# Output projection and gate as products of 64 rows, each group in its own bank over two slots

## The chip, the cores and the metric

The kernel runs on one core of a Trainium2 chip. The metric is the device time of one execution in microseconds. The engines are named as in the profile: PE (TensorE, matrix products), PEld (its weight loads), DVE (VectorE), ACT (ScalarE), POOL (GpSimd) and SP (SyncE, which issues DMAs).

## What is computed

One encoder layer over two sequences of 2048 rows of 1024 channels, with shared weights:

```python
u = _rmsnorm(h, g_norm)
z = u @ w_in
q, k, v, ga, f, gf = jnp.split(z, [int(c) for c in cuts], axis=-1)
...
a = _blocked_gqa(q, k, v) * jax.nn.silu(ga)
fo = _fourier_branch(f, w_fmix) * jax.nn.silu(gf)
h = h + jnp.concatenate([a, fo], axis=-1) @ w_out
gate = jax.nn.sigmoid(_rmsnorm(h, g_ple) @ w_ple_gate)
return h + (p @ w_ple) * gate
```

A final RMSNorm follows. Attention has 8 query heads over 2 key heads of 64 channels, without a mask.

## The kernel before

**Numbers.** A matrix product of fp32 accuracy is made of three fp16 products: each operand is split in a high and a low half, and `SPLIT3` names the pairs high x high, high x low, low x high. The helper `mm` (L433 is its matmul) runs 8 slices of 128 contracted channels times 3 products, 24 matmuls of 128 rows by 512 columns, into one PSUM bank: that is a **group**. The embedding product p @ w_ple has 2 slices, 6 matmuls.

**Stages.** First the input projection (`project`), up to some 834 us. Then attention (`attention`), a list of turns that `interleave` runs through, with a generator of other work (`fill`: the Fourier branch, then `outp`) between them. At last what is left of `outp`.

**A turn.** 64 units (sequence, key head, block of 128 queries) have 8 turns each. A turn holds six score products of 64 rows (L1126; rows 0-63 and 64-127 of PE side by side, each half in a bank of its own), two products of the running maxima for a later unit (L1153, 64 rows), then DVE's reduction of these (L1161) and ACT's two exponentials (L1129), which the scores of the turn after must wait for. Every fourth turn is heavy: it has the second attention products (L1191, 128 rows by 64 columns). In one turn of eight the sums (L1225) come, in another `max_rows` (L1177). After that the turn takes work from `fill` until its budget is spent; a generator that yields None ends its turn. `FILL` is the total that the budget is spread over. DVE work is put off by `defer` to the flush at the start of the next turn, longer DVE work by `defer_slow` to the heavy turns.

**The output projection** (`outp`), for each of 32 tiles of 128 rows: `out1` twice (the product with w_out, halves n = 0 and 1, from mh and its transposed part mT) and DVE's residual addition (L1371); `square` (ACT, L1400) and `norm`; `out2` scales the rows (ACT L1429, DVE L1433) and transposes them by DMA into hT; `out3` twice (the gate's product with w_ple_gate, ACT's tanh at L1380, the embedding product, and DVE's two operations, L1387 and L1388); a second `square`, then `out4`. The loop works on out1 of tile t, out3 of t - 1 and out4 of t - 2. `split` makes mh (ACT L1351, DVE L1356) and mT (DMA).

**Banks.** During attention the scores, maxima and second products have five of the eight PSUM banks. Three, the pool `psF`, go round among the groups, the embedding products, the sums and `max_rows`. `psX` holds five more before and after attention.

## Time and profile before

| | us |
|---|---|
| median of 3 runs | 2769.4 |
| lowest, highest | 2768.34, 2774.16 |
| the profiled execution | 2765.67 |
| its span, first to last instruction | 2763.9 |

The profile is of one execution. A row in order of time has its start, its length, engine, line and operation, the tile written and read, the shape and the number of merged instructions; matmul lengths contain the pipeline's end, so a distance between starts tells PE's rate. A wait in brackets names the idle time before and who ended it.

### The profile page before, as it was taken

Reading aid. Unit: us, or ns where it says so; the run is one execution under the profiler, and the core shown is the slowest. Engines: PE = TensorE matmul, PEld = TensorE weight load, DVE = VectorE, ACT = ScalarE, POOL = GpSimd, SP = SyncE. Lnnn points to the kernel's source line nnn. Section 1 sums busy time; section 2 is a strip of 40 time slices with the busy share of each in tenths; the row PEclk is TensorE's granted clock in tenths of the full one; section 3 lists DMA queues with packets and bytes.
Section 4 is the critical chain, followed back from the end, with each engine's and each line's share of the span. In section 5 each row is a group of like instructions: output and inputs, shape, how many; then the busy total and the mean of one; then the engine's idle time right before and its main releaser. Section 6 shows DMA issues by size and latency. Waiting matters only on the chain.

```text
span 2763.9 us, 40442 instructions
## 1 busy us (share of the span) xinstructions
PE 2674.9 (97%) x15332; PEld 1181.3 (43%) x15332; DVE 1684.7 (61%) x2467; ACT 1211.4 (44%) x2047; POOL 1630.8 (59%) x1394
## 2 busy tenths in 40 slices
PE   6899999999998989999999999999999999999998
PEld 3465655656555543333333333333333333333333
DVE  6755555654555766666666666665665665666645
ACT  3443333332224544445444544444444444444442
POOL 1233233433336697777768777777667766777770
PEclk9999999999999999999999999999999999999999
DMA  7467676774528752122222223222222222222223
GB/s 231 143 190 190 191 197 169 191 173 111 149 74 245 225 172 67 48 73 71 56 60 54 56 72 93 73 60 63 64 68 55 67 74 61 54 69 77 56 54 92
DMA packets 418532, 296.37 MB, mean 107 GB/s; under 512 B 259456, under 2 KB 360000, under 8 KB 418336
## 3 DMA queue, kind: packets, MB, share of 16 engines
q1 hardware_dynamic: 405424, 252.01, 35.0%
q0 software_dynamic: 12912, 41.77, 4.5%
q8 instruction: 120, 1.97, 0.3%
q14 instruction: 76, 0.62, 0.1%
HBM read 149.50 MB, written 86.51 MB: 85 GB/s over the span
## 4 chain that ended last, share of the span: by engine, by line
PE 78%; DVE 3%; issue 3%; DMA 2%; POOL 1%; ACT 1%; SPq 0%; DVEq 0%; POOLq 0%; ACTq 0%
PE ps_f L433 31%; PE ps_o L1191 15%; PE ps_s L1126 14%; PE ps_x L433 9%; PE ps_m L1153 4%; PE ps_f L1225 1%; PE ps_f L1177 1%; PE ps_f L1045 1%; PE ps_f L999 1%; ACT p L1129 1%; DMA hT<-h_hl 0%; DMA w_st<-in_w_out 0%; DVE a_mx L1161 0%; DMA g_in<-gd 0%; DMA w_st<-in_w_ple_gate 0%
## 5 line engine op out<-in xcount | busy, mean ns | idle before, releaser
L1134 POOL TENSOR_TENSOR acc<-acc,p 128x1024 f32<-128x1024 f32 x384 | 911.6, 2374 | 248.5 <-ACT p L1129 181.4
L1129 ACT ACTIVATE p<-ps_s,s_scale 128x512 f32<-128x512 f32 x1024 | 647.4, 683 | 753.6 <-PE ps_s L1126 736.9
L1161 DVE TENSOR_REDUCE a_mx<-ps_m 128x1 f32<-128x1024 f32 x499 | 610.2, 1223 | 593.5 <-PE ps_m L1153 592.8
L1191 PE MATMUL ps_o<-p,v 128*64 128x512 f32 x2048 | 467.5, 599 | 0.0
L433 PEld LDWEIGHTS <-uc 128*128 128x128 f16 x3072 | 301.1, 98 | 312.2 <-issue 22.5
L1126 PE MATMUL ps_s<-q,k 64*128 64x512 f16 x3072 | 424.7, 380 | 4.6 <-ACT p L1129 4.5
L433 PE MATMUL ps_f<-w_pg,hT 128*128 128x512 f16 x1464 | 351.1, 382 | 6.4 <-DMA hT<-h_hl 6.2
L1191 PEld LDWEIGHTS ps_o<-p,v 128*64 128x64 f32 x2048 | 142.2, 138 | 258.1 <-issue 249.2
L1126 PEld LDWEIGHTS <-k 64*128 64x128 f16 x3072 | 116.0, 94 | 305.1 <-issue 234.0
L433 PEld LDWEIGHTS <-hT 128*128 128x128 f16 x1536 | 138.9, 98 | 211.5 <-issue 61.0
L1132 POOL TENSOR_TENSOR acc<-p,p 128x1024 f32<-128x1024 f32 x64 | 150.5, 2352 | 111.2 <-ACT p L1129 111.1
L1153 PE MATMUL ps_m<-k,q 64*128 64x512 f16 x998 | 192.9, 378 | 16.8 <-DVE a_mx L1161 15.5
L433 PE MATMUL ps_f<-w_wo,mh 128*128 128x512 f16 x744 | 181.9, 381 | 4.6 <-DVE mh L1356 4.5
L433 PE MATMUL ps_f<-w_wo,mT 128*128 128x512 f16 x744 | 180.9, 380 | 0.0
L433 PEld LDWEIGHTS <-w_ga 128*128 128x128 f16 x1536 | 150.1, 99 | 44.1 <-issue 15.0
L915 POOL DMA_DIRECT2D gfd<-gt x32 | 19.2, 601 | 213.3 <-DVE gt L943 208.4
L1207 ACT ACTIVATE tb<-ps_o,a_scale 64x256 f32<-64x256 f32 x128 | 60.0, 469 | 165.2 <-PE ps_o L1191 164.4
L433 PE MATMUL ps_x<-uc,w_ga 128*128 128x256 f16 x1008 | 114.8, 275 | 3.8 <-ACT ge L900 3.1
L1227 DVE RECIPROCAL ps_f<-ps_f 128x256 f32<-128x256 f32 x64 | 112.4, 1756 | 7.2 <-PE ps_f L1225 7.2
L433 PEld LDWEIGHTS <-mh 128*128 128x128 f16 x768 | 68.7, 98 | 107.9 <-issue 33.2
L433 PEld LDWEIGHTS <-mT 128*128 128x128 f16 x768 | 70.0, 98 | 98.7 <-issue 25.9
L933 POOL DMA_DIRECT2D agd<-gat x64 | 35.8, 559 | 127.8 <-DVE gat L943 127.7
(283 smaller groups left out, 3322.9 us busy)
## 6 DMA issues: line engine op xcount, KB each, us to landing
q<-qTd SPq DMA_DIRECT2D x256, 64.0 KB, 2.2
ag<-agd SPq DMA_DIRECT2D x64, 256.0 KB, 4.5
out<-h POOLq DMA_DIRECT2D x31, 512.0 KB, 4.0
x<-in_x_prompt SPq DMA_DIRECT2D x16, 512.0 KB, 5.2
w_st<-in_w_out SPq DMA_DIRECT2D x32, 256.0 KB, 4.4
gfd<-gt POOLq DMA_DIRECT2D x32, 256.0 KB, 3.3
gd<-ge POOLq DMA_DIRECT2D x32, 256.0 KB, 3.4
agd<-gat POOLq DMA_DIRECT2D x64, 128.0 KB, 2.4
```

What stands on the lines that cost most here:

```text
L433: self.nc.tensor.matmul(ps, lhs(ia, k), rhs(ib, k), start=(i == 0), stop=(i == 3 * ks - 1))
L933: nc.gpsimd.dma_start(self.agd[s][1, r * 128:(r + 1) * 128, c * n:(c + 1) * n], gt[:, :n])
L999: nc.tensor.matmul(o, fT[:, r, y, :], self.bd[:, y, r, :], start=True, stop=x is None)
L1126: nc.tensor.matmul(S[u][e][:], w[sl], q[sl].rearrange("p h q -> p (h q)"), start=j == i == 0, stop=i + 1 == len(todo), skip_group_check=True)
L1129: nc.scalar.activation(p[:, e, :], S[u][e][:], AF.Exp, scale=self.sc["s_scale"][:])
L1132: nc.gpsimd.tensor_tensor(out=ACC[u][:], in0=P[u, 0][:], in1=p[:], op=ALU.add)
L1134: nc.gpsimd.tensor_tensor(out=ACC[u][:], in0=ACC[u][:], in1=p[:], op=ALU.add)
L1153: nc.tensor.matmul(ps[c], Q[u][0][sl, h, :], kt[s, kv, half][sl, :, 0, :], start=True, stop=True)
L1161: nc.vector.reduce_max(MX[u][:, h, half, c:c + 1], x, axis=AX.X)
L1191: nc.tensor.matmul(o[64 * e:64 * e + 64, :], vt[s, kv, c // 8][:, c % 8, :], p[:, e, :], start=(j == 0), stop=(j == 7))
L1207: nc.scalar.activation(tb[64 * e:64 * e + 64], ov[64 - 64 * e:128 - 64 * e, e], AF.Copy, scale=self.sc["a_scale"][64 - 64 * e:128 - 64 * e ...
L1227: nc.vector.reciprocal(r, ps[:, 0:256])
```

## The change

A group no longer runs as 24 products of 128 rows. Each product is cut into its upper 64 rows and its lower 64 rows. In one slot (`slot`, `halves`) the upper products of a new group alternate with the lower products of the group before it. Each group keeps its own bank over both slots, so it is finished a slot later than its upper half. After attention, when `psX` is there again, groups run whole.

- `psF` has one bank, the new pool `psG` two. Once `outp` has begun (`grouped`), groups take `psG`; sums, `max_rows` and embedding products take `psF`. Before that, `bank` goes round over the three as it did.
- `out1` and `out3` return the two operands and what follows the group, which runs after its lower half. The residual addition is no longer put off.
- A slot gives way after 6, 9, 12, 15, 18 and 24 steps (before: after every 3 matmuls) and ends its turn's filling with its end.
- `middle` does both squares and `norm`; `late` (out2 and out4) follows four turns later (`due`, `poll`); the loop waits for it where it needs the result (`wait`).
- `FILL` is 775 instead of 755.

```diff
-FILL = 755.0
+FILL = 775.0
...
-O4 = 6
+STOPS = (6, 9, 12, 15, 18)
...
-        self.psF = ep(tc.tile_pool(name="psF", bufs=3, space=PSUM))
+        self.psF = ep(tc.tile_pool(name="psF", bufs=1, space=PSUM))
+        self.psG = ep(tc.tile_pool(name="psG", bufs=2, space=PSUM))
+        self.grouped = False
...
         self.nx += 1
-        if self.psX is not None and self.nx % 8 < 5:
-            return self.psX.tile([128, 512], F32, name="ps_x")
-        return self.psF.tile([128, 512], F32, name="ps_f")
+        if self.grouped:
+            p, n = (self.psF, "ps_f") if self.psX is None else (self.psG, "ps_g")
+        elif self.psX is not None and self.nx % 8 < 5:
+            p, n = self.psX, "ps_x"
+        else:
+            p, n = (self.psF, "ps_f") if self.nx % (8 if self.psX is not None else 3) % 5 == 2 else (self.psG, "ps_g")
+        return p.tile([128, 512], F32, name=n)
+
+    def group_bank(self):
+
+        p, n = (self.psX, "ps_x") if self.psX is not None else (self.psG, "ps_g")
+        return p.tile([128, 512], F32, name=n)
...
+        def slot(up):
+
+
+            low = held.pop() if held else None
+            if low is not None and (low[4] or self.psX is not None):
+                j = st.tile([128, 1], F32, name="seen")
+                nc.vector.tensor_copy(j[:], low[0][:, 0:1])
+            if up is not None and self.psX is None:
+                up = (self.group_bank(), *up, not started)
+                started.append(True)
+                held.append(up)
+                yield from halves(up, low)
+            else:
+                if low is not None:
+                    yield from halves(None, low)
...
+        def halves(up, low):
 
+            i = n = 0
+            for k in range(8):
+                for ia, ib in SPLIT3:
+                    for g, sl, a, z in ((up, slice(0, 64), i == 0, False), (low, slice(64, 128), False, i == 23)):
+                        if g is not None:
+                            nc.tensor.matmul(g[0][:], g[1](ia, k)[sl], g[2](ib, k)[sl], start=a, stop=z,
+                                             skip_group_check=True)
+                    i += 1
+                    if i in STOPS:
+                        yield 0.216 * (i - n)
+                        n = i
+            n = self.nflush
+            more = low[3](low[0]) if low is not None else None
+            yield 0.216 * (24 - STOPS[-1])
+            if more is not None:
+                more()
+                yield 1.48
+            if self.dq is not None and self.nflush == n:
+                yield None
...
+        def middle(t):
+
+            ss = st.tile([128, 2], F32, name="h_ss")
...
+            if ok(t - 2):
+                yield from self.after(TK[t - 2])
+                square(t - 2, 1, ss)
+                PT.pop(t - 2)
+                HT.pop(t - 2)
+            if ok(t):
+                square(t, 0, ss)
+            q, r = norm(ss)
+
+            def late():
+                if ok(t):
+                    tk[t] = out2(t, q)
+                if ok(t - 2):
+                    t4[t - 2] = out4(t - 2, r)
+
+            due.append((self.nflush + 4, late))
```

**What stands in a row now.** On PE, in a light turn in the midst of attention, from the maxima on. Names are `k`, `q` (attention), `hT` (rows for the gate), `mh` (rows for the output projection), `w_pg`, `w_wo` (weights). Before:

```order
L1153 MATMUL ps_m<-k_7165,q_13005 128x512 [waits DVE_49]
L1153 LDWEIGHTS q_13005 [waits DMAHW7_49]
L1153 MATMUL ps_m<-k_7165,q_13005 128x512
L433 LDWEIGHTS hT
L433 MATMUL ps_f<-w_pg_9874,hT 128x512
```

And now:

```order
L1164 MATMUL ps_m<-k_7168,q_12396 128x512 [waits DVE_49]
L1164 LDWEIGHTS q_12396
L1164 MATMUL ps_m<-k_7168,q_12396 128x512
L1445 LDWEIGHTS hT [waits DMAHW1_49]
L1445 MATMUL ps_g<-w_pg_9388,hT 128x512
L1445 LDWEIGHTS mh
L1445 MATMUL ps_g<-w_wo_8988,mh 128x512
```

Where one group's load and product repeated, a gate group's upper half (rows 0-63) and an output group's lower half (rows 64-127) alternate, in two banks of `ps_g`.

On PE, in a turn with `max_rows` that follows a turn with an embedding product. Before:

```order
L1153 MATMUL ps_m<-k_7168,q_13005 128x512 [waits DVE_49]
L1153 LDWEIGHTS q_13005
L1153 MATMUL ps_m<-k_7168,q_13005 128x512
L1177 MATMUL ps_f<-ident,nm 128x128
L433 LDWEIGHTS mh
L433 MATMUL ps_f<-w_wo_8660,mh 128x512 [waits Activation_49]
```

And now:

```order
L1164 MATMUL ps_m<-k_7171,q_12973 128x512 [waits DVE_49]
L1164 LDWEIGHTS q_12973
L1164 MATMUL ps_m<-k_7171,q_12973 128x512
L1188 MATMUL ps_f<-ident,nm 128x128 [waits DVE_49]
L1445 LDWEIGHTS mh
L1445 MATMUL ps_g<-w_wo_8988,mh 128x512
```

The product of `max_rows` now waits for DVE; what it waits for in the built program is the second operation on the embedding product (L1407), which reads the same bank.

On ACT, around the squares of a tile in the second half of attention (`p` are the exponentials, `th` the tanh, `tb` a copy after a heavy turn, `nm` the negated maxima). Before:

```order
L1380 ACTIVATE th<-ps_f,h_pg_6890 128x512
L1129 ACTIVATE p_16180<-ps_s,s_scale 128x512 x2
L1400 ACTIVATE h_hl,h_ss<-h 128x1024
L1129 ACTIVATE p_16241<-ps_s,s_scale 128x512 x2
L1207 ACTIVATE tb<-ps_o,a_scale 64x256 x2
```

And now:

```order
L1182 ACTIVATE nm<-a_m_17107 128x2x4
L1466 ACTIVATE sq,h_ss<-h 128x1024
L1466 ACTIVATE h_hl,h_ss<-h 128x1024
L1140 ACTIVATE p_17241<-ps_s,s_scale 128x512 x2
L1140 ACTIVATE p_17267<-ps_s,s_scale 128x512 x2
```

The two squares of a step of the loop stood at two places, with exponentials between them, and stand together now.

## Rows read from the trace of the kernel before

**Rows 1.** The profile's page: busy time, the granted clock of TensorE in 40 slices, and the chain that ended last, by engine and by line.

```profile
PE 2674.9 (97%) x15332; PEld 1181.3 (43%) x15332; DVE 1684.7 (61%) x2467; ACT 1211.4 (44%) x2047; POOL 1630.8 (59%) x1394
...
PEclk9999999999999999999999999999999999999999
...
PE 78%; DVE 3%; issue 3%; DMA 2%; POOL 1%; ACT 1%; SPq 0%; DVEq 0%; POOLq 0%; ACTq 0%
PE ps_f L433 31%; PE ps_o L1191 15%; PE ps_s L1126 14%; PE ps_x L433 9%; PE ps_m L1153 4%; PE ps_f L1225 1%; PE ps_f L1177 1%; PE ps_f L1045 1%; PE ps_f L999 1%; ACT p L1129 1%; DMA hT<-h_hl 0%; DMA w_st<-in_w_out 0%; DVE a_mx L1161 0%; DMA g_in<-gd 0%; DMA w_st<-in_w_ple_gate 0%
```

**Rows 2.** Busy time by stretch: attention with the Fourier branch, attention with the output projection, the rest. After the stretch and its length, the busy us of each engine (and its instructions), TensorE's granted clock, the DMA share and GB/s.

```profile
834.00:1062.00 228.00, 202.53 (x1343) 110.06 (x1340) 142.33 (x179) 116.36 (x193) 170.16 (x108) 0.95 0.65 199
1062.00:2690.00 1628.00, 1613.75 (x8990) 577.58 (x8989) 1012.79 (x1047) 783.99 (x1304) 1183.37 (x1007) 1.00 0.25 64
2690.00:2764.00 74.00, 64.17 (x298) 27.98 (x295) 39.15 (x88) 16.97 (x26) 10.89 (x10) 0.95 0.37 91
```

**Rows 3.** PE in order of time: a light turn and the start of the heavy turn after it.

```profile
1341.21 0.82 PE L1126 MATMUL ps_s<-q,k 64*128 64x512 f16 x6
1341.87 0.38 PE L1153 MATMUL ps_m<-k,q 64*128 64x512 f16 x2
1342.18 2.12 PE L433 MATMUL ps_f<-w_pg,hT 128*128 128x512 f16 x9
1344.23 0.82 PE L1126 MATMUL ps_s<-q,k 64*128 64x512 f16 x6
1344.89 0.38 PE L1153 MATMUL ps_m<-k,q 64*128 64x512 f16 x2
1345.20 0.65 PE L1225 MATMUL ps_f<-acc,ones 128*64 128x256 f32 x4
```

**Rows 4.** PE in order of time after attention: a whole group of the gate and what follows it.

```profile
2704.80 5.34 PE L433 MATMUL ps_f<-w_pg,hT 128*128 128x512 f16 x24
2709.98 1.46 PE L433 MATMUL ps_x<-wp,pT 128*128 128x512 f16 x6
```

**Rows 5.** PE in order of time in the input projection: two groups of 256 columns.

```profile
485.75 2.78 PE L433 MATMUL ps_f<-uc,w_ga 128*128 128x256 f16 x24
488.37 2.78 PE L433 MATMUL ps_x<-uc,w_ga 128*128 128x256 f16 x24
```

**Rows 6.** PE in order of time: the start of a turn and its `max_rows`, and later an embedding product at the end of a turn and the start of the next.

```profile
1324.04 0.82 PE L1126 MATMUL ps_s<-q,k 64*128 64x512 f16 x6
...
1325.00 0.49 PE L1177 MATMUL ps_f<-ident,nm 128*128 128x128 f32 x2
...
1329.64 1.46 PE L433 MATMUL ps_f<-wp,pT 128*128 128x512 f16 x6
1331.03 0.39 PE L1126 MATMUL ps_s<-mr,kone 64*128 64x512 f16 x2
```

**Rows 7.** DVE in order of time in the same turns: the reduction, the reading of the `max_rows` bank, and the two operations on the embedding product.

```profile
1325.12 1.23 DVE L1161 TENSOR_REDUCE a_mx<-ps_m 128x1 f32<-128x1024 f32 x1 [1.15 <-PE ps_m L1153]
1326.26 0.68 DVE L1179 TENSOR_TENSOR mr<-ps_f,own 128x512 f16<-128x512 f32 x1
...
1331.20 0.70 DVE L1387 SCALAR_TENSOR_TENSOR ps_f<-th,ps_f 128x512 f32<-128x512 f32 x1 [1.53 <-PE ps_f L433]
1331.93 0.75 DVE L1388 SCALAR_TENSOR_TENSOR h<-ps_f,p_wp,h 128x512 f32<-128x512 f32 x1
```

**Rows 8.** ACT in order of time: a square with the reading of its accumulator and the exponentials behind it, and the exponentials of the turn that starts at 1344.23.

```profile
1338.05 1.05 ACT L1400 ACTIVATE h_hl<-h 128x1024 f16<-128x1024 f32 x1
1339.00 0.20 ACT L1400 ACTIVATION_READ_ACCUMULATOR h_hl<-h 128x1 f32 x1
1339.09 1.26 ACT L1129 ACTIVATE p<-ps_s,s_scale 128x512 f32<-128x512 f32 x2
...
1345.15 1.26 ACT L1129 ACTIVATE p<-ps_s,s_scale 128x512 f32<-128x512 f32 x2 [1.75 <-PE ps_s L1126]
```

**Rows 9.** PE in order of time at the start of attention: the first score product of three turns, two of them without filling.

```profile
835.56 0.37 PE L1126 MATMUL ps_s<-q,k 64*128 64x512 f16 x1 [0.54 <-ACT p L1129]
...
837.52 0.37 PE L1126 MATMUL ps_s<-q,k 64*128 64x512 f16 x1 [0.36 <-ACT p L1129]
...
839.48 0.37 PE L1126 MATMUL ps_s<-q,k 64*128 64x512 f16 x1 [0.36 <-ACT p L1129]
```

**Rows 10.** Who waited for whom from 1066 to 2690 us: us in total, times, longest.

```profile
PEld L433 <- DMA hT<-h_hl: 9.7, 7, 3.0
...
PE ps_f L433 <- DMA hT<-h_hl: 6.2, 4, 2.5
...
PE ps_f L433 <- DVE mh L1356: 4.5, 3, 1.7
```

**Rows 11.** One of DVE's groups by line and shape, the residual addition, from 1100 to 2650 us: busy us, mean ns of one, idle time before.

```profile
L1371 DVE SCALAR_TENSOR_TENSOR h<-ps_f,mixo,h 128x512 f32<-128x512 f32 x54 | 40.2, 745 | 4.2 <-PE ps_f L433 4.2
```

**Rows 12.** The end of the program in order of time: the last product and the last output.

```profile
2752.71 1.46 PE L433 MATMUL ps_x<-wp,pT 128*128 128x512 f16 x6
...
2760.24 1.00 SPq L1421 DMA_DIRECT2D out<-h  x2
```

More of the change, by code (lines that the diff above doesn't have):

```diff
@@ new lines, in slot @@
+        def slot(up):
[11 more added lines that the diff above has]
+                    yield from halves(None, low)
+                if up is not None:
+                    ps = self.group_bank()
+                    yield from self.mm(ps[:], up[0], up[1])
+                    more = up[2](ps)
+                    if more is not None:
+                        more()
+                        yield 1.28
@@ new lines, in halves @@
+        def halves(up, low):
[13 more added lines that the diff above has]
+            yield 0.216 * (24 - STOPS[-1])
+            if more is not None:
+                more()
+                yield 1.48
+            if self.dq is not None and self.nflush == n:
+                yield None
@@ L1459, in along, with poll, wait @@
             for us in g:
-                next(pr, None)
+                for _ in range(round(us / 0.648) if us else 0):
+                    next(pr, None)
+                poll()
                 yield us
+        def poll():
+            while due and (self.dq is None or self.nflush >= due[0][0]):
+                due.pop(0)[1]()
+        def wait(d, t):
+            while t not in d:
+                yield None
+                poll()
+            yield from self.after(d.pop(t))
+        def middle(t):
+            ss = st.tile([128, 2], F32, name="h_ss")
+            if not (ok(t) and ok(t - 2)):
+                nc.gpsimd.memset(ss[:], 1.0)
+            if ok(t - 2):
[12 more added lines that the diff above has]
+            due.append((self.nflush + 4, late))
+            if self.dq is None:
+                poll()
         mix = []
@@ L1476, in outp @@
         load_x(0)
-        t4, tm = [-1], []
+        held, started, due, tm, tk, t4 = [], [], [], [], {}, {}
+        self.grouped = True
         for t in range(N2 + 2):
-            ss = st.tile([128, 2], F32, name="h_ss")
-            if not (ok(t) and ok(t - 2)):
-                nc.gpsimd.memset(ss[:], 1.0)
             pr = prep(t + 1) if ok(t + 1) else iter(())
             if ok(t):
-                yield from along(out1(t, 0), pr)
-            if ok(t - 2):
-                yield from self.after(tf)
-                square(t - 2, 1, ss)
-            if ok(t):
-                yield from along(out1(t, 1), pr)
+                yield from along(slot(out1(t, 0)), pr)
+                if t == 1:
+                    yield from middle(0)
+                yield from along(slot(out1(t, 1)), pr)
+                load_p(t)
@@ L1506, in outp @@
-            if self.dq is not None and ok(t - 1):
-                yield from self.after(tn, 3)
-            if o4:
-                t4 = out4(t - 2, r)
-            if ok(t - 1):
-                PT.pop(t - 1)
-                HT.pop(t - 1)
-                tf = TK[t - 1]
-            if t == 0:
-                for _ in range(4):
-                    yield None
-            if ok(t):
-                tk = out2(t, q)
+                yield from wait(tk, t - 1)
+                yield from along(slot(out3(t - 1, 0)), pr)
+            elif t:
+                yield from along(slot(None), pr)
@@ L1519, in outp @@
+            if t:
+                yield from middle(t)
+            if ok(t - 1):
+                yield from along(slot(out3(t - 1, 1)), pr)
             if ok(t + 1):
-                yield from self.after(t3)
+                if ok(t - 3):
+                    yield from wait(t4, t - 3)
                 load_x(t + 1)
```

59 lines of the change are left out of this document (25 added, 34 removed).

## Prediction

> **What bounds the kernel now.** I read the page's first part and its chain before anything else [rows 1]: the TensorE (PE) is busy 97% of the span and the chain that ended last is 78% PE, while the next engine, DVE, stands at 61%. So only what shortens PE's row, or makes it wait, can move the time. Then the busy time by stretch [rows 2]: from 1062 to 2690 us, where attention and the output projection run side by side, PE is busy 1613.8 of 1628 us at a granted clock of 1.00 (the 2.4 GHz level). "Busy" is not yet "at its rate", since a matmul's end is modelled; so I went to PE's own rows in order of time [rows 3] and took the distance from start to start. In the last stretch 24 products of the gate take 5.18 us, 0.216 us each [rows 4]. In a turn of attention, 1341.21 to 1344.23, there are three steps of scores (six 64-row products, two side by side, 0.22 us a pair), one step of maxima (two side by side) and nine 128-row products: 13 steps of 0.216 us are 2.81 us, but the turn took 3.02. The 0.21 us left over lie at the two places where PE goes from 64-row to 128-row products and back: maxima to gate 0.31 instead of 0.22, and nine products in 2.05 instead of 1.94. **One change of form costs 0.106 us**, and no other engine is named there. That is what this change aims at.
>
> **Removed.** With 64-row products on both sides, scores, maxima and projection no longer differ in form. Counting the matmuls of both built programs, PE changes between 64-row, 128-row and 64-column forms 1044 times before and 582 times after. 462 x 0.106 = **-49.0 us**. What is left is at the attention's second products (L1191), the sums, the running maxima (L1177) and the embedding product (L433 wp), which keep their forms.
>
> **Added products.** 121 of the 128 groups become 24 upper and 24 lower halves. Of their 2928 steps 2880 hold a pair and 48 hold one half (the first group's upper rows, the last one's lower). Before, they were 121 x 24 = 2904 steps. 24 more x 0.216 = **+5.2 us**. I take a pair at 0.216, as the score pairs run [rows 3]. A pair issues two weight loads and two products. The nearest long run with that density is the 256-wide projection, 24 loads and 24 products in 2.62 us [rows 5], 0.109 for one load and one product, so 0.218 a pair: the upper end is 2880 x 0.002 = +6 us. Nothing makes a pair cheaper than its 0.216 of moving columns, so the lower end is 0.
>
> **The banks.** Before, sums, maxima, embedding and groups rotate through three banks. After, groups hold two for two slots and the other three share one. Whoever takes that one waits until DVE has finished with its last user.
> - Embedding at the end of a turn, then sums or maxima in the next: in the built order 16 times. The embedding ends with the turn; DVE's two operations on it start 0.17 us into the next turn (1331.20 against 1331.03) and end 1.65 us in [rows 6, 7]. Sums or maxima want the bank 0.96 us in [rows 6]. 0.73 x 16 = +11.7 us. Behind the waiting product stand the second products or the pairs of that turn, so nothing hides it.
> - Maxima, then an embedding in the same turn: 8 times. DVE reads the maxima's bank only after its reduction, until 2.90 us into the turn (1326.26 + 0.68, turn at 1324.04) [rows 6, 7]; four embeddings want it at 1.29 (wait 1.6 to 1.7), four at 2.69 (0.2 to 0.3): +7.7 us.
> - A group's bank: the next slot starts at the earliest 0.87 us into a turn, and the residual operation, 0.745 us on DVE [rows 11], cannot start before the group's last product ends, some 0.17 us in. That is 0.11 us late, at 31 places where a light turn goes straight to the pairs: +3.4 us; at no place less than 0, at all 45 +5.
>
> Together +22.8 us. Rows and rule can be weighed here. The rows show the three users of a shared bank and when DVE lets go of it. The Trainium skill, in TensorEngine Tiling (Array Packing), "Gotcha 1: PSUM Pressure", warns that row tiles raise the demand for banks, which speaks against taking the 49 us as the gain. Without the first two items, which are that pressure, the sum below would be 2731 us; with them it is what I forecast. No run here shows yet how large it is.
>
> **The scalar engine.** A turn's exponentials start 0.92 us in and end 2.18 us in [rows 3, 8], and the next but one turn's scores need them. A turn with no filling lasts 1.96 us [rows 9] though PE has only 0.87 us of work. Two edits bear on this. (1) The two squares, which stood at two places, now follow each other: 2 x 1.04 us (1338.05 to 1339.09) [rows 8]. For each pair of squares I compared 2.18 + 2.08 + 1.26 = 5.5 us with the length of its turn and the next, counted in steps: these are too short at five places, by 0.01 to 1.6 (there a copy of mh follows as well), in sum +3 us. Lower end 0, upper end the same pair at nine places, +9. (2) The group's end closes a turn's filling, and the waits for the normalised rows are by ticket: eleven light turns get no filling (or the running maxima alone), where six did before. 5 x 1.1 = +5.5 us (0 if the next turn's work covers it).
>
> **Weights of rows that come late.** PE's loads wait for hT seven times, 9.7 us, and its products for mh three times, 4.5 us [rows 10]. hT's second half is now issued at least two turns ahead but for the first tile, where eight were issued in the same turn or the one before: -9.7 us (0 if the transposing DMA is slower). mh's lower half is used in the turn in which it is made at five places instead of one in one and two in the next; at 1.5 us each (4.5 / 3) [rows 10] 7.5 instead of 4.5: +3.0.
>
> The tail keeps seven groups in 128-row form, and its last chain, from the last product at 2752.71 to the output [rows 12], is the same. FILL and the finer stops only set in which turn a product stands; that is in the counts above.
>
> **Sum.** -49.0 + 5.2 + 22.8 + 3 + 5.5 - 9.7 + 3.0 = -19.2 us. Against the profiled execution, 2765.7 us, that is 2746.5; that execution lies 3.7 us under the median of the runs, so the forecast is 2769.4 - 19.2 = **2750.2 us**.
>
> **Rivals.**
> - *The waits take it.* All waits at their upper ends: the second kind of bank wait always 1.66 (+5.6), nine pairs of squares (+6), 45 group banks (+1.6), hT as late as before (+9.7): 2773 us. For it: each engine has little slack in a light turn. Against it: DVE is at 61%, and a late PE gives ACT its time back.
> - *Waits overlap.* A wait at a bank also lets the exponentials catch up; half of the 34.3 us of new waits (22.8 + 3 + 5.5 + 3.0): 2733 us. For it: both sit in the same short turns. Against: the bank waits stand on PE's own path.
> - *Slower: a long run of pairs costs more than a score pair.* The rows show at most five pairs in a row; there the first pair costs 0.01 us more, three score steps taking 0.66 instead of 0.65 [rows 3]. If loads cannot keep ahead in runs of 6 to 12 pairs and every pair pays that 0.011, it is 2880 x 0.011 = +32 us: 2782 us. It decides from 19.2 / 2880 = 0.0067 us a pair on, where the gain is gone. Against it: [rows 5], where loads hold up at the same density. The Trainium skill, in TensorE: Matmul & The Clock Gate, "Wait — 56ns, not 53.3ns?", gives about 62 ns of sequencer work per matmul in one decoding mode; two are 124 ns and fit in a pair, but if loads paid it too, 248 ns a pair would be some 92 us more (an estimate from that page). The 109 ns for a load and a product in [rows 5] does not agree with that.
> - *It does not do what it says:* PE pays the change between upper and lower halves of different banks anyway. 2750.2 + 49 = 2799 us. The scores go to the maxima, other banks and other weights, with no such gap [rows 3].
>
> **How the numbers follow.** Forecast 0.61, waits at the upper end 0.12, overlap 0.20, slower pairs 0.05, no effect 0.02. A measurement here can tell about 0.2% (5.5 us) from no change. Faster by more: the forecast's and the overlap's chance but for a few hundredths, 0.80; within: most of the upper-end case, 0.13; slower: 0.07. The range leaves out the two slow cases, most of the upper end and the better half of the overlap: 2733 to 2767.
>
> **What would show it.** Light turns with pairs and no other form should last 13 steps, 2.81 us, not 3.02; a run of pairs should go at 0.216 each. The sums and maxima that follow an embedding should wait for DVE, 0.7 us each; embeddings after maxima 1.6. PE's waits for hT should be gone. I am wrong if a pair takes 0.22 or more, if a change of form still shows between maxima and pairs, or if PE's waits add up to far more or less than 35 us.

## Result: no gain, some 0.2% slower

| | before | after |
|---|---|---|
| median | 2770.3 us | 2776.0 us |
| lowest, highest | 2763.0, 2774.2 | 2772.5, 2778.6 |
| the profiled execution's span | 2763.9 | 2773.5 |

The ratio is 1.0022, 95% interval 1.0013 to 1.0032. The forecast was 2750.2 us in a range of 2733 to 2767: the time lies above the range, on the other side of no change.

**The profile after.** The page's first part and its chain, against [rows 1]: PE still sets the time, but DVE has grown from 3% to 7% of the chain.

```profile
PE 2656.9 (96%) x18236; PEld 1264.5 (46%) x18236; DVE 1684.4 (61%) x2469; ACT 1214.7 (44%) x2047; POOL 1636.9 (59%) x1394
...
PE 83%; DVE 7%; issue 3%; DMA 2%; POOL 2%; ACT 2%; SPq 0%; DVEq 0%; POOLq 0%; ACTq 0%
```

PE in order of time in a light turn, which answers to [rows 3]:

```profile
1849.35 0.81 PE L1137 MATMUL ps_s<-q,k 64*128 64x512 f16 x6
1849.99 0.38 PE L1164 MATMUL ps_m<-k,q 64*128 64x512 f16 x2
1850.21 0.38 PE L1445 MATMUL ps_g<-w_pg,hT 64*128 64x512 f16 x1
1850.21 0.38 PE L1445 MATMUL ps_g<-w_wo,mh 64*128 64x512 f16 x1
...
1851.94 0.38 PE L1445 MATMUL ps_g<-w_pg,hT 64*128 64x512 f16 x1
...
1852.15 0.81 PE L1137 MATMUL ps_s<-q,k 64*128 64x512 f16 x6
```

From scores to scores 2.80 us for 13 steps, where 3.02 stood before. From maxima to pairs 0.22, no longer 0.31. Nine pairs from 1850.21 to 1852.15, 0.216 each. The change does what it says, and the form changes are saved.

**Where the time went.** I cut both profiled executions at the first score product of attention and at that of its last turn. A step is one 128-row product or one pair of 64-row products. Losses are a turn's length less 0.216 us a step and 0.106 a form change, summed over the turns from PE's starts.

| us | before | after | difference |
|---|---|---|---|
| until attention (833.76, 844.80) | 833.8 | 844.8 | +11.0 |
| attention, 511 turns | 1854.2 | 1840.3 | -13.9 |
| of it steps and form changes | 1793.8 | 1745.0 | -48.8 |
| of it losses | 60.5 | 95.2 | +34.7 |
| from there to the end of the span | 75.9 | 88.4 | +12.5 |

Attention has the -49, and waits take 35 of it. But 23.5 us come in the two stages for which the sum had next to nothing: the projection ahead of attention, whose instructions are the same in the same order, and the tail.

PE's rows of who waited for whom from 1066 us to the end of attention, against [rows 10] (us in total, times, longest):

```profile
PE ps_s L1137 <- ACT p L1140: 6.5, 19, 0.7
...
PE ps_f L1236 <- DVE h L1407: 6.2, 8, 0.8
PE ps_f L444 <- DVE mr L1190: 6.0, 4, 1.5
...
PE ps_f L1188 <- DVE h L1407: 5.8, 9, 0.7
...
PE ps_g L1445 <- DVE mh L1367: 2.3, 4, 0.8
...
PE ps_g L1445 <- DMA hT<-h_hl: 2.2, 1, 2.2
```

The second to fourth are the one shared bank `ps_f`: 18.0 us in 21 waits, none of which stood in the trace before.

The projection, PE in order of time, and below it two stretches of 2 us (busy us of PE, PEld, DVE, ACT, POOL with their instructions, granted clock, DMA share, GB/s):

```profile
286.83 2.78 PE L444 MATMUL ps_g<-uc,w_ga 128*128 128x256 f16 x24
293.96 5.28 PE L444 MATMUL ps_g<-uc,w_ga 128*128 128x256 f16 x24 [4.35 <-DVE gat L954]
```

```profile
294.00:296.00 2.00, 2.00 (x10) 1.39 (x10) 0.96 (x2) 0.00 (x0) 0.54 (x1) 0.50 0.80 297
296.00:298.00 2.00, 2.00 (x12) 1.35 (x10) 0.00 (x0) 0.00 (x0) 0.00 (x0) 0.50 0.23 87
```

A group waits 4.35 us for DVE to read the group just before it, since both have the same bank of `ps_g`; then its 24 products take 5.28 us instead of 2.78, at a granted clock of 0.50 (the 1.2 GHz level).

The tail, PE and DVE in order of time, and PE's clock in the stretch:

```profile
2707.22 0.39 PE L444 MATMUL ps_x<-w_pg,hT 128*128 128x512 f16 x1
2710.57 8.16 PE L1445 MATMUL ps_g<-w_pg,hT 64*128 64x512 f16 x24 [2.96 <-DVE seen L1422]
2718.66 2.74 PE L444 MATMUL ps_g<-wp,pT 128*128 128x512 f16 x6
```

```profile
2709.16 1.28 DVE L1367 SCALAR_TENSOR_TENSOR mh<-ag,mix_s,mh 128x1024 f16<-128x1024 f32 x1 [7.55 <-ACT mh L1362]
2710.36 0.15 DVE L1422 COPY seen<-ps_g 128x1 f32<-128x1 f32 x1
```

```profile
2710.50:2718.60 8.10, 8.03 (x24) 2.81 (x23) 5.29 (x18) 2.30 (x3) 0.71 (x2) 0.65 0.29 55
2718.60:2721.20 2.60, 2.60 (x8) 0.87 (x8) 0.00 (x0) 0.69 (x1) 0.00 (x0) 0.50 1.10 231
```

The last group's lower half runs alone. The kernel holds it back until its own upper half is done in the bank that both share: a copy on DVE (`seen`) stands between them, and on DVE this copy is queued behind the last tile's mh. PE is idle for 2.96 us, and the granted clock falls behind that: 0.65 in the mean over the 24 products, which take 8.16 us, and 0.50, the lower level, over the six products of the embedding, which take 2.74 instead of 1.46 [rows 4].

### The profile page after: what moved, and what is told of

The parts are those of the page before. It is cut to its first block, busy times and chain, and to the rows that moved or that the text cites. A ratio compares the mean times of both kernels' runs of the same rounds, so it can differ in the third digit from the quotient of the medians.

```text
span 2773.5 us, 46318 instructions
## 1 busy us (share of the span) xinstructions
PE 2656.9 (96%) x18236; PEld 1264.5 (46%) x18236; DVE 1684.4 (61%) x2469; ACT 1214.7 (44%) x2047; POOL 1636.9 (59%) x1394
## 3 DMA queue, kind: packets, MB, share of 16 engines
q1 hardware_dynamic: 405424, 252.01, 34.7%
## 4 chain that ended last, share of the span: by engine, by line
PE 83%; DVE 7%; issue 3%; DMA 2%; POOL 2%; ACT 2%; SPq 0%; DVEq 0%; POOLq 0%; ACTq 0%
PE ps_g L1445 22%; PE ps_o L1202 15%; PE ps_x L444 14%; PE ps_s L1137 12%; PE ps_f L444 6%; PE ps_g L444 6%; PE ps_m L1164 3%; DVE a_mx L1172 1%; PE ps_f L1236 1%; PE ps_f L1188 1%; ACT p L1140 1%; POOL acc L1145 1%; PE ps_g L1056 1%; DVE h L1407 1%; DVE ps_f L1405 1%
## 5 line engine op out<-in xcount | busy, mean ns | idle before, releaser
L1445 PE MATMUL ps_g<-w_pg,hT 64*128 64x512 f16 x2832 | 507.8, 378 | 5.4 <-DVE seen L1422 3.0
L1137 PE MATMUL ps_s<-q,k 64*128 64x512 f16 x3072 | 438.7, 378 | 7.6 <-ACT p L1140 7.4
L1445 PEld LDWEIGHTS <-hT 64*128 64x128 f16 x2832 | 206.2, 94 | 169.4 <-issue 19.7
L1445 PE MATMUL ps_g<-w_wo,mh 64*128 64x512 f16 x1488 | 269.6, 378 | 3.6 <-DVE mh L1367 2.3
L1137 PEld LDWEIGHTS <-k 64*128 64x128 f16 x3072 | 148.8, 94 | 261.2 <-issue 140.5
L1445 PE MATMUL ps_g<-w_wo,mT 64*128 64x512 f16 x1488 | 264.5, 376 | 0.4 <-DMA mT<-mh 0.3
L1164 PE MATMUL ps_m<-k,q 64*128 64x512 f16 x998 | 205.1, 377 | 16.6 <-DVE a_mx L1172 15.7
L1445 PEld LDWEIGHTS <-mh 64*128 64x128 f16 x1488 | 101.7, 94 | 97.9 <-issue 17.4
L1445 PEld LDWEIGHTS <-mT 64*128 64x128 f16 x1488 | 107.2, 94 | 81.2 <-DMA mT<-mh 1.3
L944 POOL DMA_DIRECT2D agd<-gat x64 | 35.9, 561 | 134.1 <-DVE gat L954 134.0
L1238 DVE RECIPROCAL ps_f<-ps_f 128x256 f32<-128x256 f32 x60 | 105.4, 1756 | 7.6 <-PE ps_f L1236 7.6
```

What stands on the lines that cost most here:

```text
L944: nc.gpsimd.dma_start(self.agd[s][1, r * 128:(r + 1) * 128, c * n:(c + 1) * n], gt[:, :n])
L1137: nc.tensor.matmul(S[u][e][:], w[sl], q[sl].rearrange("p h q -> p (h q)"), start=j == i == 0, stop=i + 1 == len(todo), skip_group_check=True)
L1164: nc.tensor.matmul(ps[c], Q[u][0][sl, h, :], kt[s, kv, half][sl, :, 0, :], start=True, stop=True)
L1238: nc.vector.reciprocal(r, ps[:, 0:256])
L1445: nc.tensor.matmul(g[0][:], g[1](ia, k)[sl], g[2](ib, k)[sl], start=a, stop=z, skip_group_check=True)
```

## Experiments

Stages of all kernels, from their profiles, and the ratio to the kernel before:

| | until attention | attention | tail | median | ratio (95%) |
|---|---|---|---|---|---|
| before | 833.8 | 1854.2 | 75.9 | 2770.3 | |
| after | 844.8 | 1840.3 | 88.4 | 2776.0 | 1.0022 (1.0013, 1.0032) |
| before_again | 838.4 | 1853.8 | 75.9 | 2768.4 | 0.9998 (0.9989, 1.0008) |
| after_again | 844.0 | 1843.3 | 90.5 | 2778.3 | 1.0028 (1.0017, 1.0039) |
| tail_first | 845.3 | 1844.1 | 80.4 | 2768.5 | 0.9997 (0.9989, 1.0006) |
| three_banks | 836.4 | 1840.6 | 80.4 | 2762.6 | 0.9970 (0.9958, 0.9982) |
| before_banks | 844.7 | 1872.9 | 75.9 | 2795.5 | 1.0092 (1.0078, 1.0106) |
| free_rows | 845.1 | 1861.8 | 89.7 | 2795.7 | 1.0090 (1.0073, 1.0108) |
| rows_first | 841.2 | 1842.4 | 89.5 | 2776.6 | 1.0027 (1.0018, 1.0037) |
| sums_after | 849.8 | 1858.0 | 88.6 | 2798.8 | 1.0104 (1.0090, 1.0118) |
| embed_apart | 837.8 | 1836.1 | 80.4 | 2758.5 | 0.9963 (0.9950, 0.9976) |
| fill_755 | 837.5 | 1811.2 | 108.4 | 2758.3 | 0.9957 (0.9943, 0.9970) |
| rows_early | 837.7 | 1855.4 | 80.4 | 2772.7 | 1.0010 (1.0001, 1.0019) |
| sums_late | 835.3 | 1886.9 | 80.4 | 2806.6 | 1.0141 (1.0124, 1.0158) |

**Both kernels once more** (no edit).

> The kernel before, unchanged, profiled once more. It asks whether the 11 us by which attention starts later in the profile of the changed kernel (844.8 us against 833.8) is the change's doing or scatter between executions: the code up to there computes the same in both, and the profile after shows single waits at banks there (4.35 us at 289.6, and TensorE at its lower level for some 4 us behind it). Theory A (scatter: a bank that comes free late in some executions): this profile's attention starts anywhere from 834 to 845 us, not at 834 again, and the times of the kernel before alone spread over some 10 us. Theory B (the changed program is slower there by itself): attention starts within 2 us of 833.8 in this profile and the ratio is 1.000 within 0.001.

> The changed kernel, unchanged, profiled once more, for the same question from the other side. Theory A (scatter): attention starts away from 844.8 us by several us, between 834 and 845, while the attention stage (1840.3 us from the first score product to the last turn's) and the tail (88.4 us) come out within 1 us of the first profile. Theory B (systematic): attention starts at 844 to 846 us again. The ratio should be 1.002 again in either case (1.001 to 1.004).

Neither theory is right as written. Before, attention starts at 833.8 and 838.4, so there is scatter; after, at 844.8 and 844.0, and no profile of one meets the other. That points to the change, and three_banks below shows it. Attention's 1843.3 and the tail's 90.5 show some 2 to 3 us of scatter in those stages.

**tail_first.** After attention the next whole group goes ahead of the single lower half:

```diff
-                if low is not None:
-                    yield from halves(None, low)
                 if up is not None:
                     ps = self.group_bank()
                     yield from self.mm(ps[:], up[0], up[1])
-                    more = up[2](ps)
+                if low is not None:
+                    yield from halves(None, low)
+                more = up[2](ps) if up is not None else None
...
```

> The changed kernel, but after attention a slot runs the new whole group first and the left-over lower half behind it, so that DVE's short copy of the bank (L1422), for which the 24 single products waited 2.96 us, is done beside the whole group. Theory A (the 12.5 us by which the tail is longer are 24 more steps, this wait, and TensorE's lower level of 1.2 GHz behind it): the wait goes, the single half runs at 0.22 us a product (5.2 instead of 8.16 us), and the tail is 80 to 83 us long instead of 88.4; time 5 to 8 us less than the changed kernel, ratio to before 0.999 to 1.001. Rival (the last tile's chain, sums to mh, sets the end of the tail anyway): the wait moves to the products of the last tile and the tail stays at 87 to 89 us; ratio 1.002.

PE in order of time there:

```profile
2711.52 4.27 PE L444 MATMUL ps_x<-w_pg,hT 128*128 128x512 f16 x19
2715.72 5.35 PE L1445 MATMUL ps_g<-w_pg,hT 64*128 64x512 f16 x24
```

No wait, and 5.35 us for the 24. The tail is 80.4, as theory A says; the time, 2768.5, is 7.5 us under the changed kernel's 2776.0 and 9.8 under its 2778.3 in after_again, where 5 to 8 were expected. The rival falls. What is left of the tail's 12.5 us, 4.5, is 18 more steps and six more form changes, the 24 steps of the lone half among them.

**three_banks.** One pool of three until attention, and tail_first's tail:

```diff
-        self.psF = ep(tc.tile_pool(name="psF", bufs=1, space=PSUM))
-        self.psG = ep(tc.tile_pool(name="psG", bufs=2, space=PSUM))
+        self.three = ExitStack()
+        self.psF = self.psG = self.three.enter_context(tc.tile_pool(name="psF3", bufs=3, space=PSUM))
...
         self.psX = None
+        self.three.close()
+        self.psF = self.ep(pool("psF", 1, space=PSUM))
+        self.psG = self.ep(pool("psG", 2, space=PSUM))
```

> The changed kernel with the tail as in tail_first, and with one pool of three banks until attention, as the kernel before has it; the split into one and two banks begins with attention. So each group of the projection gets the bank that it has in the kernel before. Four profiles of programs with the split show attention starting at 844.0 to 845.3 us, two of the kernel before at 833.8 and 838.4, so the scatter theory is weakened. Theory A (the split itself: a pool of two banks, one of them still held, hands out the bank of the group just before, as at 289 us, where PE waited 4.35 us for DVE and then ran at 1.2 GHz): attention starts at 833 to 839 us, the tail stays at 80 to 81, time 2760 to 2762 us, ratio to before 0.996 to 0.998. Rival (the longer program, or something else in it that is not the banks): attention starts at 844 to 845.5 us again, time 2768 to 2769, ratio 0.999 to 1.001.

Attention starts at 836.4: theory A, with a time 0.6 us above its range. Over all runs, seven profiles with three banks in the projection start it at 833.8 to 838.4 (mean 836.7), seven with the split at 841.2 to 849.8 (mean 845.0). The split costs 8.3 us in a stage in which nothing else differs. The reason stands in the built programs. A bank whose tile is still in use is passed over. With three, the next group takes another free one; with two and one, at the place near 290 us the only free bank of the pool was that of the group just before: the two groups have bank 2 one after the other, where the kernel before and three_banks give them banks 0 and 2. The wait there stands in all seven profiles with the split, 1.2 to 5.1 us long (0 to 2.1 with three banks), and two more of some 1.0 us, near 490 and 740 us, stand in these seven alone.

**before_banks.** The kernel before, with groups whole, in the changed kernel's banks:

```diff
         def out1(t, n):
-            ps = self.bank()
+            ps = self.group_bank()
...
-            ps = self.bank()
+            ps = self.group_bank()
             yield from self.mm(ps[:], lambda b, k: HT[t][:, b, k, :], lambda b, k: ow[f"pg{n}"][b][:, k, :])
...
+        self.grouped = True
```

> The kernel before with the changed kernel's banks alone: groups whole, in two banks of their own, and sums, max_rows and embedding in the third; before attention the same split as in the changed kernel. Theory A (the split of the banks costs by itself what the forecast's bank waits and the projection say): attention starts at 844 to 845.5 us, new waits of 12 to 20 us in attention (1866 to 1874 instead of 1854), the tail is 76 as before; ratio to before 1.007 to 1.010. Rival (the bank waits come from the pairs' schedule, in which a group's end closes a turn, and hardly stand here): attention less than 4 us longer, ratio 1.003 to 1.004.

Theory A in all numbers. Attention is 18.9 us longer, and the rows of who waited for whom on PE there show the shared bank:

```profile
PE ps_f L444 <- DVE mr L1190: 7.7, 9, 1.5
...
PE ps_f L1236 <- DVE h L1399: 7.5, 10, 1.1
...
PE ps_f L1188 <- DVE h L1399: 5.2, 8, 0.9
```

So the banks alone cost some 27 us by the stages (8 and 19) and 25.5 by the times (0.92%). Against this kernel the pairs shorten attention by 31 us (1872.9 to the 1842.1 that is the mean of the four profiles with the changed kernel's attention).

**free_rows and rows_first.** Can the waits at the shared bank be had back by freeing it earlier? free_rows has both edits, rows_first only the second:

```diff
-                        nc.vector.scalar_tensor_tensor(out=pp[:], in0=th[:], scalar=1.0, in1=pp[:], op0=ALU.add,
+                        nc.vector.scalar_tensor_tensor(out=th[:], in0=th[:], scalar=1.0, in1=pp[:], op0=ALU.add,
                                                        op1=ALU.mult)
-                        nc.vector.scalar_tensor_tensor(out=x[:, sl], in0=pp[:], scalar=h, in1=x[:, sl],
+                        nc.vector.scalar_tensor_tensor(out=x[:, sl], in0=th[:], scalar=h, in1=x[:, sl],
...
+            turn(g)
             self.drain(lead(g))
...
                 pv((g - 1) // 8, (g - 1) % 8 - PVG + 1)
-            turn(g)
```

> The changed kernel with the shared bank given back earlier at two places: DVE's first operation on an embedding product writes its result over the tanh in SBUF instead of into the bank, so the bank is free 0.73 us earlier; and max_rows is issued ahead of the maxima, so that DVE reads its bank ahead of the 1.2 us reduction. Everything computed is the same. Theory A (bank waits on PE's own path: 18.0 us in the profile after, 6.2 at the sums, 5.8 at max_rows, 6.0 at the embedding): the waits at the sums and at max_rows go and those at the embedding fall from 1.65 to about 0.4 each; attention is 15 to 18 us shorter than 1840.3, time 2758 to 2761, ratio to before 0.995 to 0.997. Rival (what PE waits for at the bank gives the exponentials and DVE time that they need, so other waits take the place): attention is 0 to 8 us shorter, ratio 0.999 to 1.002.

> The changed kernel with one of the two edits of free_rows alone: max_rows ahead of the maxima of its turn, so DVE reads that bank ahead of its 1.2 us reduction; the embedding's two DVE operations are as in the changed kernel. In free_rows attention got 20 us longer though the waits at the bank fell by 15, and DVE's second operation on the embedding (L1407), with both operands in SBUF, took 1.58 us in the mean instead of 0.75. Theory A (that operation is what lost the time): here it is 0.75 us again, the four waits of 1.66 us at the embedding fall to about 0.5 (-4.6), the eight at max_rows grow by the 0.22 us of the maxima (+1.8); attention is 0 to 4 us shorter than 1840 to 1844, ratio to before 1.001 to 1.003. Rival (DVE's reduction, now behind max_rows' operation, holds up the next turn's maxima): attention is 8 us or more longer, ratio 1.005 or more.

free_rows missed by far: the waits at the bank went as expected, and attention grew by some 20 us. The groups of DVE by line and shape (busy us, mean ns, idle before), the embedding's second operation after and in free_rows, and DVE in order of time in free_rows:

```profile
L1407 DVE SCALAR_TENSOR_TENSOR h<-ps_f,p_wp,h 128x512 f32<-128x512 f32 x56 | 42.1, 751 | 2.0
```

```profile
L1407 DVE SCALAR_TENSOR_TENSOR h<-th,p_wp,h 128x512 f32<-128x512 f32 x54 | 85.3, 1579 | 1.9
```

```profile
1931.78 2.65 DVE L1407 SCALAR_TENSOR_TENSOR h<-th,p_wp,h 128x512 f32<-128x512 f32 x1
1934.35 0.68 DVE L1190 TENSOR_TENSOR mr<-ps_f,own 128x512 f16<-128x512 f32 x1
1934.95 1.21 DVE L1172 TENSOR_REDUCE a_mx<-ps_m 128x1 f32<-128x1024 f32 x1
```

One of POOL's additions beside it, and PE's longest sum of waits in free_rows:

```profile
1931.52 2.35 POOL L1145 TENSOR_TENSOR acc<-acc,p 128x1024 f32<-128x1024 f32 x1
```

```profile
PE ps_m L1164 <- DVE a_mx L1172: 35.9, 33, 5.1
```

With one operand in PSUM each of the 56 takes 0.75 us; with both in SBUF 0.75 to 2.96, and the long ones are those beside POOL's additions. Here the addition ends at 1933.87 and the operation at 1934.43, 0.55 us later; of the 42 in the whole execution that take over 0.9 us, 40 end 0.55 us after the addition that ran when they began. The reduction behind it is late, and the next maxima wait 1.66 us for it. Over attention the waits for the reduction are 35.9 us, where they were 15.7, and those for mh 9.1 instead of 2.3: more than the bank gave back. The Trainium skill, in SBUF — State Buffer, "SBUF: two separate sides", states that a DVE operation with two inputs in SBUF and a GpSimd operation that reads SBUF lock each other out of a shared pair of ports; this trace agrees. In rows_first the operation is at 0.75 us again, the waits at the embedding fall from 6.0 to 1.8 us, those at `max_rows` grow from 5.8 to 8.0, and attention is 1842.4: theory A, with no gain worth the name.

**sums_after.** The sums behind the second products:

```diff
-            if j == 4 and 0 <= u - 1 < n:
-                sums(u - 1)
...
                 pv((g - 1) // 8, (g - 1) % 8 - PVG + 1)
+            if j == 4 and 0 <= u - 1 < n:
+                sums(u - 1)
```

> The changed kernel with the sums issued behind the second products of their turn instead of ahead of them. The same work in another order, and the same number of form changes. Theory A (bank waits on PE's path are lost time): the eight waits of 0.84 us at the sums go, since 3.6 us of second products stand ahead of them now; attention is 6 to 8 us shorter than its 1840 to 1844 us, ratio to before 0.999 to 1.001 (the changed kernel's is 1.002 to 1.003). Rival (the wait gives the exponentials and DVE the time that they need): other waits take its place, attention is less than 2 us shorter, ratio 1.002 to 1.003.

Worse than both theories. PE, then DVE, in order of time around one such turn:

```profile
1318.28 0.60 PE L1236 MATMUL ps_f<-acc,ones 128*64 128x256 f32 x4
...
1321.65 1.47 PE L444 MATMUL ps_f<-wp,pT 128*128 128x512 f16 x6 [1.79 <-DVE at L1239]
```

```profile
1319.39 1.75 DVE L1238 RECIPROCAL ps_f<-ps_f 128x256 f32<-128x256 f32 x1
1321.17 0.42 DVE L1239 TENSOR_TENSOR at<-at,ps_f 128x256 f32<-128x256 f32 x1
1321.51 1.22 DVE L1172 TENSOR_REDUCE a_mx<-ps_m 128x1 f32<-128x1024 f32 x1
```

The waits at the sums are gone. But the reciprocal, 1.75 us, now runs in the light turn behind, ahead of that turn's reduction in DVE's queue, and the embedding of that turn wants the bank: waits for the reduction go from 15.7 to 27.3 us over attention, and the embedding waits 9.2 us for L1239.

**embed_apart and fill_755.** three_banks with a rule: an embedding is put off by a turn where the shared bank would be wanted at once, and `max_rows` goes a turn earlier unless an embedding has just been. fill_755 sets FILL to 755 in that.

```diff
             if more is not None:
+                while self.dq is not None and self.clash(self.step):
+                    yield None
                 more()
+                self.emb = self.step
...
+            for a in (3, 2):
+                v, k = divmod(g + a, 8)
+                if k == 0 and 0 <= v < n and v not in done and (a == 2 or 0 <= g and self.emb != g - 1):
+                    max_rows(v)
...
+        def clash(g):
+            v, k = divmod(g + 3, 8)
+            return (self.rows == g or (g + 1) % 8 == 4 and 0 <= (g + 1) // 8 - 1 < n
+                    or k == 0 and v < n and v not in done)
```

> three_banks with a rule in place of an edit on DVE: an embedding product is put off to the next turn when the shared bank would be wanted at once (max_rows in the same turn, sums or max_rows in the next), and max_rows is issued a turn earlier unless an embedding has just been. In the built order no embedding is then followed by sums or max_rows in the next turn (22 times in three_banks) or preceded by max_rows in its own turn (9 times); DVE's operations, their operands and the form changes stay. Theory A (the 18 to 20 us of waits at the shared bank are time lost on PE's own path, and in free_rows and sums_after it was a longer operation or a wait in DVE's queue that lost more than they gave): attention is 14 to 20 us shorter than three_banks' 1840.6, time 2743 to 2749 us, ratio to before 0.990 to 0.993. Rival (the waits give the exponentials and DVE time that they need in any order): attention 1836 us or more, ratio 0.995 to 0.998.

> embed_apart with the pacing of the kernel before (FILL 755 instead of 775): some 20 us of products move from attention into the tail, in which they run as whole groups of 128 rows without a change of form. Theory A (pacing only sets in which turn a product stands): attention 18 to 22 us shorter and the tail as much longer than in embed_apart; time within 4 us of it. Rival (the fuller turns of 775 are what makes single waits show, at hT, mh and the exponentials): 5 to 10 us faster than embed_apart, from fewer waits in attention; or slower by as much, if the lighter turns leave PE waiting for the exponentials.

PE's waits in embed_apart over attention:

```profile
PE ps_s L1138 <- ACT p L1141: 16.9, 52, 0.8
...
PE ps_f L1189 <- DVE at L1240: 1.8, 1, 1.8
...
PE ps_f L445 <- DVE mr L1191: 0.6, 3, 0.2
```

Of 18.0 us at the shared bank 2.4 are left, yet attention is only 4.5 us shorter: waits for the exponentials rose from 8.8 to 16.9. The result lies at the rival's end. Pacing is theory A, though more was moved than it says: attention 24.9 shorter, the tail 28.0 longer, the medians 0.2 us apart. These two are the fastest versions here, 0.9963 and 0.9957.

**rows_early and sums_late.** three_banks with the earlier `max_rows` alone, as in the loop above, and then also:

```diff
-            if j == 4 and 0 <= u - 1 < n:
+            if 0 <= u - 1 < n and (j == 4 and self.emb != g - 1 or j == 5 and u - 1 in AT):
                 sums(u - 1)
```

> three_banks with max_rows a turn earlier unless an embedding has just been issued; embeddings are not put off, so no turn loses filling. It asks why embed_apart got only 4.5 us of attention for 16 us of bank waits that went: because waits at the bank had given ACT its time (Rival), or because its rule emptied turns, whose length ACT's exponentials then set (waits for them 16.9 us instead of 8.8; Theory A). In the built order embeddings followed by max_rows in the next turn go from 12 to 0, max_rows followed by an embedding in its own turn from 9 to 12. Theory A: the 5.8 us of waits at max_rows go, three more meetings in one turn give back up to 5.0 (3 x 1.66), waits for the exponentials stay at 9 to 10 us; attention is 1 to 6 us shorter than 1840.6 and at least two thirds of the bank waits' balance shows in it. Rival: the waits for the exponentials grow by as much as the bank waits shrink, attention 1839 to 1842 us whatever the balance.

> rows_early, and the sums go into the next (light) turn where an embedding has just been issued, 10 of 56 times, so that no embedding is followed by sums either. Theory A: the 6.2 us of waits at the sums go; attention 4 to 7 us shorter than in rows_early; ratio to before 0.993 to 0.996. Rival (as in sums_after: DVE's reciprocal of 1.76 us, now in a light turn, holds up the reduction, and PE waits for that): waits for the reduction grow by 5 us or more, attention no shorter than in rows_early.

Attention is 14.8 us longer in rows_early than in three_banks, slower than both theories, and 31.5 longer still in sums_late: no shorter, as its rival says, but not by the rival's way, for the waits for the reduction fell there from 21.0 to 16.1. PE's waits in rows_early, then in sums_late with one wait of the ten and PE's clock behind it:

```profile
PE ps_m L1165 <- DVE a_mx L1173: 21.0, 16, 4.9
...
PE ps_f L445 <- DVE mr L1191: 14.3, 9, 2.9
...
PE ps_s L1138 <- ACT p L1141: 8.9, 27, 0.7
```

```profile
PE ps_f L1189 <- DVE at L1240: 28.5, 10, 3.0
```

```profile
1481.35 0.77 PE L1189 MATMUL ps_f<-ident,nm 128*128 128x128 f32 x2 [2.96 <-DVE at L1240]
```

```profile
1481.40:1484.20 2.80, 2.80 (x14) 1.21 (x16) 0.69 (x1) 0.00 (x0) 2.72 (x2) 0.50 0.19 52
```

In rows_early the waits at `max_rows` for the embedding are gone and those for the exponentials stay at 8.9, as theory A says. But nine embeddings now meet `max_rows` in their own turn and wait 1.6 us each, and the reduction is waited for 5.6 us more. In sums_late I had put the sums into the very turn in which the earlier `max_rows` stands: ten of these wait, nine of them 2.96 us. The waits move from one of the three users to the next. And a long wait costs more than its length: none of the four 1.5 us waits in the changed kernel is followed by a lower granted clock, but seven of the nine of 2.96 us in sums_late are. From 1066 us on, attention runs 41 us at 0.50 in sums_late and 14 in rows_early, against 3 in the changed kernel; half of that is lost.

For embed_apart the traces can be compared with three_banks turn by turn. Putting off an embedding ends a turn's filling: twelve turns that have an embedding in three_banks have no filling there and lose 7 us more (0.78 at turns 171 and 227, where nothing was lost before), and four turns behind them lose 2 more. That is 9 of the 12 us by which the turns that wait for the exponentials got longer, so its rule brought most of these waits.

## Why the prediction was wrong

- **Removed: right.** Steps and form changes fell by 48.8 us in attention and rose by 4.5 in the tail, -44.3; the prediction has -49.0 + 5.2 = -43.8.
- **Pairs: right.** 2530 distances from pair to pair, wherever nothing waited, are 0.2162 us in the mean. The rival of slow pairs needed 0.0067 more, the rival of no effect a gap between maxima and pairs; both fall.
- **The banks: right in attention.** 21 waits of 18.0 us by the wait rows, 19.7 by starts, against 19.4 for the first two items. By starts it is 0.84 us at the sums, 0.74 at `max_rows` and 1.65 at four embeddings; the other four lose 0.14, where 0.2 to 0.3 were forecast, and the longer waits at the sums make up for it. before_banks shows that the split alone does this. The rows that the prediction names give 1.65 - 0.96 = 0.69 and 2.90 - 1.29 = 1.61; its 0.73 and 1.66 add 0.04 to 0.05 that it has no row for. The third item was too small: small losses (0.05 to 0.16 us a turn), which are mostly of this kind, went from 3.0 to 8.9 us, +5.9 against 3.4. Its own rows give 0.17 + 0.745 - 0.87 = 0.045 and not 0.11; measured are some 0.15, for in 15 light turns the pairs start 0.36 us after the maxima instead of 0.21.
- **hT: mis-sized.** The sum takes off all 9.7 us, though the same sentence excepts the first tile. That tile still costs some 4.5 us, in turn 64: PE waits for it, and behind the wait a pair takes 0.43 us at a granted clock of 0.50. Besides, the 9.7 are waits of the loads (PEld); PE itself stood idle for 6.2 [rows 10].
- **Scalar engine: the right order of size; mh: the wrong way.** Waits for the exponentials rose by 5.5 us (1.0 to 6.5 from 1066 us on) against 8.5; mh fell by 2.2 instead of rising by 3.0.
- **The waits in attention: +34.7 us where the terms gave 24.6.** I put each turn's loss down to the longest wait in it, from turn 60 on. That gives +20.2 us at the shared bank, +6.6 in losses under 0.17 us, +7.3 for the exponentials, +2.0 for DVE's reduction and some +4 at other places, for which the sum had no term; -4.4 for hT and -0.5 for mh. So the 10 us that the sum lacks are hT (5), the banks (4) and what had no term (6), less 5 for mh and the exponentials.
- **"The tail keeps seven groups in 128-row form, and its last chain ... is the same": failed.** I compared the last chain and not the last pair's way out. The lone half was counted; the wait in front of it (2.96 us) and the lower clock behind it (8.16 - 5.35 and 2.74 - 1.46 us) were not, 7 us. tail_first takes them away.
- **No term for the projection: failed.** The sum took the banks ahead of attention as going round as they did before. They do not, and that is 8.3 us in the mean of all profiles. three_banks takes it away.

The first tile's wait for hT in turn 64, PE in order of time, and a stretch behind it:

```profile
1101.91 0.61 PE L1445 MATMUL ps_g<-w_pg,hT 64*128 64x512 f16 x1 [2.15 <-DMA hT<-h_hl]
```

```profile
1102.00:1105.00 3.00, 3.00 (x16) 1.06 (x18) 0.00 (x0) 0.00 (x0) 0.00 (x0) 0.50 0.24 46
```

Steps in their own terms: 10 us more waits in attention, 7 in the tail, 8 in the projection, 25 in all, which is what lies between the forecast -19.2 and the +5.7 of the medians. The two profiles alone lie +9.6 apart, with a few us of scatter between executions.

Of the rivals, *the waits take it* came nearest in time, 2773, but by another way: 15 of the 25 us lie outside the stage that it speaks of. *Waits overlap* is not what made the result. embed_apart, where 16 us fewer waits at the bank were worth 4.5, looks like it, but there the turns without filling took most of the gain; how much a wait at the bank gives back to the exponentials is not shown.

With tail and projection mended the change does gain: three_banks is 7.5 us (0.30%) faster than the kernel before, 2762.6. It is still 12 us above the forecast, 10 of it by the waits in attention.

## What to carry to other kernels

When a pool of banks is split, look at every stage that draws from it, those before the change too: a pool of three could pass over a busy bank here, one of two gave out the bank of the group just before. Where a pipeline of halves ends, ask what orders the last half behind its own partner, and which queue that order stands in. Work moved on DVE to spare PE a wait is worth it only if nothing that PE needs stands behind it there, as the reduction did in free_rows and sums_after.

## What had not been expected of the hardware

That DVE's time for one operation hangs on where its operands lie and on what POOL does meanwhile, as free_rows shows, was one surprise; that freeing the bank earlier by order alone gains so little, as rows_first shows, was another. The third: here the two row halves of PE do not wait for each other. Where only upper halves run ahead of the scores (PE in order of time, after), the scores' lower rows start beside the last upper products:

```profile
1045.23 0.39 PE L1137 MATMUL ps_s<-q,k 64*128 64x512 f16 x1
1045.44 0.38 PE L1445 MATMUL ps_g<-w_wo,mT 64*128 64x512 f16 x1
1045.46 0.38 PE L1137 MATMUL ps_s<-q,k 64*128 64x512 f16 x1
1045.65 0.38 PE L1445 MATMUL ps_g<-w_wo,mT 64*128 64x512 f16 x1
```

Products that come later in the program begin 0.2 to 0.4 us ahead of earlier ones on the other half; the turn before, with 28 steps, took 5.41 us, 0.64 less than its steps.
